# A bidirectional RWKV-7 and latent-attention block: two PSUM banks for each pair of copies in the scan, a scratch of its own for each token tile, and constants later

## The chip, the core and the metric

The kernel runs on one core of a Trainium2 chip. TensorE multiplies, VectorE and ScalarE move results out of PSUM and do elementwise work, GpSimd (POOL) does a little elementwise work, and SyncE (SP) issues the loads of weights. PSUM, where TensorE writes, is used here as eight banks of 128 partitions x 512 float32. The metric is the device time of one execution in microseconds; of a kernel the median of several runs is taken.

## The reference

One encoder layer over 256 tokens of 2048 channels, float32:

```python
h = rms_norm(x, g_pre)
proj = h @ w_in                       # 2048 x 10688
mla_in, rwkv_in, z_mla, z_rwkv, gate_mla, gate_rwkv = split(proj)
# branch 1: latent attention, 8 heads, q and kv through ranks 512
y_mla = mla_attention(q_nope, q_rope, k_nope, k_rope, v_mla)
# branch 2: RWKV-7, 16 heads of 64, one scan forwards and one backwards
rin = rin + rwkv_mu * (centred_shift(rin) - rin)
#   step: sa = st @ a_t; st = st * w_t + sa b_t^T + v_t k_t^T; y = st @ r_t
y = rwkv7_bidir_scan(r, w_f, w_b, k_f, k_b, v, kk, a_f, a_b)
y_rwkv = group_norm(y) + bonus
u_mla = (y_mla * silu(z_mla)) @ w_br_mla
u_rwkv = (y_rwkv * silu(z_rwkv)) @ w_br_rwkv
merged = sigmoid(gate_mla) * u_mla + sigmoid(gate_rwkv) * u_rwkv
x = x + rms_norm(merged @ w_out, g_post)
```

## The kernel before

All large products are made as three products of float32r parts: ScalarE rounds a chunk of weights to its high part (`whi`, L331), VectorE subtracts to get the low part (`wlo`, L334), and TensorE multiplies high by high, high by low and low by high (L400 to L402). A chunk is 128 x 1024 or less; three raw buffers and three split buffers go round. These are the *main matmuls*.

**A planner writes the order.** Nothing is scheduled on the chip: each engine runs its instructions in the order in which they are issued. The order comes from `Streams` (L45), a small simulation. Each part of the kernel is a generator that yields requests such as `("A", cost, ready, table)`, with `P`, `A`, `D`, `G`, `S` for TensorE, ScalarE, VectorE, GpSimd and SyncE. The planner grants the engine that can start first, and among requests that could start within a slot the one with the lowest rank; only then the generator issues its instructions. `W` waits for a condition, `T` for a time. `cA(n)` and `cD(n)` are the costs assumed for n elements on ScalarE and VectorE, `S0` is when loads are assumed to begin, and a yielded number such as `0.73 * n` for a piece of x is an assumed cost. So a changed number changes the order of issue and nothing else. The waits between engines are put in by the framework from the tiles that instructions read and write.

**PSUM.** Three banks (`DB`) serve the main matmuls, five (`MB`) all smaller ones; `take` waits until one is free and `give` returns it.

**The start** (`start`, L1402). x comes in pieces of 256 columns (`dma_stream`, L277). `row(t)` sums the squares of token tile t in four pieces: tile 0 on ScalarE, tile 1 on VectorE (`SQ`), each writing the squares, which nobody reads, to `junk[:, i]`, the same piece for both tiles. Then come sum, root and reciprocal (`rs`), and x is scaled piece by piece on ScalarE, VectorE or GpSimd (`SC`). `turned` transposes x by TensorE, and `ev_h` (L1448) brings each block of h into SBUF in two parts: ScalarE `hhi` (L1452), VectorE `hlo` (L198). The first eight blocks are multiplied unscaled and `ev_first` multiplies by the reciprocals that `spread` laid along the free axis. The constants (four small VectorE operations, L1500 to L1503, which make `vd`, `ka1` and change `vec`) are made as soon as the second reciprocal is there; `mix` (L421) is their first reader.

**The RWKV branch** goes in four quarters Q of four heads, both directions at once, so eight head-states `st`. `front_d`, `front_k`, `front_v` and `bonus` prepare a quarter; `front_d` contains the decay's running sum (`tensor_tensor_scan`, L702). `chunks_of(Q)` (L771) makes the Gram matrices, and inverts a triangular 64 x 64 matrix per chunk of 64 tokens: 32 x 32 blocks on VectorE, then two joins (L856 to L874), each of 32 small matmuls into one bank and four copies of 32 partitions, alternately on ScalarE and VectorE. Then it walks through four chunks q, and in each: `by_v` and the state's products give the right sides in `pu` (one bank; half of the heads on partitions 0 to 63, half on 64 to 127); ScalarE copies the one half (L921) and VectorE the other (L923) into `rhs`; 16 matmuls (L928) solve for U, into `pu` again; ScalarE (L930) and VectorE (L932) copy U into `uv`; then follow the new state (L946), y (L949) and the next chunk's `by_v`. Main matmuls are issued between these steps.

Of the kernel before, what the change touches and what calls it, by code (L numbers as in the profile page):

```python
# [15 lines left out]
S = 256  # L16
D = 2048
# [8 lines left out]
SLOT = {'P': 0.03, 'A': 0.06, 'D': 0.08, 'G': 0.1, 'S': 0.1}  # L26
S0 = 1.5
LATE = 0.3
# [130 lines left out]
def encoder_block_kernel(  # L159
# [117 lines left out]
    def dma_stream():  # L277
# [5 lines left out]
        while True:  # L283
            for what, k, n in before.get(i, ()):
                if what == "x":
                    e = yield ("S", 0.73 * n, 0.0)
                    C = slice(256 * k, 256 * (k + n))
                    nc.sync.dma_start(xt[:, :, C], xv[:, :, C])
                    for kp in range(k, k + n):
                        have["xl", kp] = e  # L290
                else:
                    have["kr", k] = yield ("S", 0.182 * n, 0.0)
                    o = krw[k // 8][:, 0:512].rearrange("p (k c) -> p k c", k=8)
                    nc.sync.dma_start(o[:, k % 8:k % 8 + n], w_in_v[:, k:k + n, 1024:1088])
            yield ("W", lambda: i < len(chunks) and i < done["split"] + NRAW)
            c = chunks[i]
            c.t = yield ("S", 0.55 if i < 2 else 1.1 if i < 9 else 1.46, O.free["D"] if i > 9 else 0.0)
            c.load(raws[i % NRAW])
# [122 lines left out]
    def mix(p, m, mcol, o):  # L421

        q = yield from QP.take()
        for j in range(2):
# [238 lines left out]
    def front_d(Q, d):  # L663
# [36 lines left out]
        act.activation(w65(lw)[:, :, :, 1:65], v4(rv(w2d(th))), AF.Copy, bias=-0.5 * KAPPA, scale=-0.5 * KAPPA)  # L700
        yield ("D", cD(520))
        dve.tensor_tensor_scan(out=fl(th), data0=scanm, data1=fl(lw), initial=0.0, op0=ALU.mult, op1=ALU.add)  # L702
# [68 lines left out]
    def chunks_of(Q):  # L771
# [84 lines left out]
        for step in range(2):  # L856

            m = yield from MB.take()
            pm = m[:, 0:256].rearrange("p (u c) -> p u c", u=8)
            e = yield ("P", 0.5, None, "32x32")  # L860
            for u in range(32):
                j = 32 * (u % 4)
                o = pm[j:j + 32, u // 4]
                if step == 0:
# [3 lines left out]
            for j in range(4):  # L868
                on, cost = (("A", cA(256) + 0.07), ("D", cD(256) + 0.09))[j % 2]
                yield (on, cost, e)  # L870
                copy = act.copy if on == "A" else dve.tensor_copy
                copy(tm[B2, j::4] if step == 0 else Gu[B1, j::4, 32:64], pm[32 * j:32 * j + 32])
            MB.give(m)
            yield ("T", max(O.free["A"], O.free["D"]))  # L874
# [18 lines left out]
        def by_v(pu, q):  # L893

            for dj in range(4):
                for h in range(2):
                    pe.matmul(pu[R64[1 - h], dj], G[:, 2 * dj + h, q, 0:64], z.uv[q][:, 2 * dj + h], start=dj == 0,
                              stop=(dj == 3 and q == 0))

        for q in range(4):  # L900
# [3 lines left out]
            if q == 0:  # L904
                mu = yield from MB.take()
                pu = mu[:, 0:256].rearrange("p (a c) -> p a c", a=4)
                e = yield ("P", 0.48, None, "128x64")
                by_v(pu, q)
            m = yield from MB.take()
            py = m[:, 0:256].rearrange("p (a c) -> p a c", a=4)  # L910
            if q:
                e = yield ("P", 0.5, None, "64x64")

                for dj in range(4):
                    ar = z.ar[dj // 2][:, dj % 2, q]
                    for h in range(2):
                        pe.matmul(pu[R64[1 - h], dj], ar[R64[h], 0:64], Z[R64[h], dj], start=False, stop=dj == 3)
                    for h in range(2):
                        pe.matmul(py[R64[h], dj], Z[R64[h], dj], ar[R64[h], 64:128], start=dj == 0, stop=False)
            e0 = yield ("A", cA(256) + 0.08, e)  # L920
            act.copy(rhs[Hs, 1], pu[R64[0]])  # L921
            e1 = yield ("D", cD(256) + 0.11, e)
            dve.tensor_copy(rhs[Hs, 0], pu[Hs])  # L923
            e = yield ("P", 0.48, max(e0, e1), "64x64")
            for a in range(4):
                for i in range(2):
                    st = 4 * i + a
                    pe.matmul(pu[R64[i], a], G[Hs, st, q, 0:64], rhs[Hs, st % 2, st // 2], start=a == 0, stop=a == 3)  # L928
            e1 = yield ("A", cA(256) + 0.08, e)
            act.copy(uv[Hs, 0:4], pu[R64[0]])  # L930
            e2 = yield ("D", cD(256) + 0.11, e)
            dve.tensor_copy(uv[Hs, 4:8], pu[Hs])  # L932
            MB.give(mu)
            eu = max(e1, e2)
            ez = eu
            Zn = Z
            m2 = (yield from MB.take()) if q < 3 else None
            mu = (yield from MB.take()) if q < 3 else None
            cost = 1.0 if q < 3 else 0.5
# [10 lines left out]
            if q < 3:  # L950
                pu = mu[:, 0:256].rearrange("p (a c) -> p a c", a=4)
                by_v(pu, q + 1)
# [449 lines left out]
    def start():  # L1402
        junk = sb([128, 4, 512], "b8", 1)
        sq = sb([128, 2, 4], "sq")
# [13 lines left out]
        def row(t):  # L1418
            e = []
            for i in range(4):  # L1420
# [74 lines left out]
        O.add(turned([*range(UN // 2, 8), *range(UN // 2)], "x", "h"), 0)  # L1495
        O.add(spread(), 1)
        yield ("W", lambda: ("rs", 1) in have)

        yield ("D", 0.5)
        ts(vd, vec, 0.5, 0.0)  # L1500
        ts(ka1, vd[:, V_KA:V_KA + 8], -1.0, 1.0)
        ts(vec[:, V_MU:V_MUL + 4], vec[:, V_MU:V_MUL + 4], -1.0, 1.0)
        ts(vd[:, V_KK:V_KK + 8], vec[:, V_KK:V_KK + 8], -1.0, 0.0)  # L1503
        yield ("W", lambda: done["dma"] >= 8)
        yield ("A", 0.25, 26.0)
# [147 lines left out]
```

## Time and profile before

| | |
|---|---|
| median of 3 runs | 866.34 us (866.2 to 866.93) |
| profiled execution | 866.99 us |
| its span, first to last instruction | 865.2 us |
| TensorE busy | 843.4 us (97%) |
| VectorE busy | 660.1 us (76%) |
| ScalarE busy | 501.0 us (58%) |
| mean granted TensorE clock | 0.997 of full speed |

Busy is the time in which an engine had an instruction under way. In rows of the trace PE is TensorE, PEld its weight loads, DVE VectorE, ACT ScalarE. `m` and `d` are banks of `MB` and `DB`, and tiles are named without their numbers. A bracket such as `[0.74 <-DVE work L923]` says that the engine stood idle for 0.74 us before the instruction, and what ended that.

### The profile page before, as it was taken

The numbers are of one execution on the slowest core, as the hardware profiler recorded it, in microseconds if no ns is written. First come the engines' busy times: TensorE is split into PE (matmuls) and PEld (weight loads), VectorE is DVE, ScalarE is ACT, GpSimd is POOL, SyncE is SP. The second block draws the span as 40 slices with busy tenths as digits, with TensorE's granted clock in tenths as the row PEclk, the third lists the DMA queues.
The fourth block names the chain that finished last, engine by engine and source line by source line (L and its number), as shares of the span: only waits on it lengthen the run. The fifth ranks groups of instructions, "written<-read, shape, count | busy, mean of one in ns | idle before, by whom it ended". The sixth has DMA issues, their size and how long they took to land.

```text
span 865.2 us, 19404 instructions
## 1 busy us (share of the span) xinstructions
PE 843.4 (97%) x8112; PEld 807.4 (93%) x8112; DVE 660.1 (76%) x1082; ACT 501.0 (58%) x797; POOL 31.8 (4%) x66
## 2 busy tenths in 40 slices
PE   8899999999999999999999999999999999999996
PEld 8899999999999989999999999899999999998884
DVE  5887798869997869887878988766777766765554
ACT  6678654477654587644678444657766543544442
POOL 4210000000000000000010000000000000000000
PEclk9999999999999999999999999999999999999998
DMA  8566646544366624366532566454663575555563
GB/s 273 160 183 169 178 125 183 161 132 123 108 181 185 173 82 117 104 199 178 152 102 77 151 191 174 118 139 159 178 200 112 164 247 191 180 188 193 195 204 113
DMA packets 123528, 139.41 MB, mean 161 GB/s; under 512 B 6704, under 2 KB 110512, under 8 KB 123056
## 3 DMA queue, kind: packets, MB, share of 16 engines
q1 hardware_dynamic: 121664, 135.16, 53.0%
q0 software_dynamic: 768, 1.57, 0.6%
q10 hardware_dynamic: 1008, 1.44, 0.5%
q8 instruction: 63, 1.03, 0.5%
q14 instruction: 25, 0.20, 0.1%
HBM read 136.05 MB, written 2.10 MB: 160 GB/s over the span
## 4 chain that ended last, share of the span: by engine, by line
PE 87%; DVE 7%; ACT 3%; issue 1%; DMA 1%; SPq 0%; POOL 0%; DVEq 0%; ACTq 0%
PE d L400 20%; PE d L402 19%; PE d L401 19%; PE m L1333 2%; PE m L1334 2%; PE m L1335 2%; PE m L801 2%; DVE wlo L334 1%; PE m L402 1%; PE m L400 1%; PE m L401 1%; PE d L1334 1%; PE d L1333 1%; PE d L1335 1%; DVE work L195 1%
## 5 line engine op out<-in xcount | busy, mean ns | idle before, releaser
L331 ACT CAST whi<-raw 128x1024 fp32r<-128x1024 f32 (+3 forms) x252 | 253.1, 1006 | 247.7 <-PE d L401 165.5
L400 PE MATMUL d<-hhi,whi 128*128 128x256 f32 (+1 forms) x1328 | 384.4, 289 | 0.0
L334 DVE TENSOR_TENSOR wlo<-raw,whi 128x1024 fp32r<-128x1024 f32 (+3 forms) x250 | 292.5, 1172 | 116.3 <-ACT whi L331 114.2
L402 PE MATMUL d<-hhi,wlo 128*128 128x256 f32 (+1 forms) x1328 | 375.4, 283 | 1.3 <-DVE wlo L334 1.3
L401 PE MATMUL d<-hlo,whi 128*128 128x256 f32 (+1 forms) x1328 | 375.2, 283 | 0.0
L400 PEld LDWEIGHTS d<-hhi,whi 128*128 128x128 f32 (+1 forms) x1328 | 253.0, 191 | 4.1
L402 PEld LDWEIGHTS d<-hhi,wlo 128*128 128x128 f32 (+1 forms) x1328 | 253.2, 191 | 1.6 <-DVE wlo L334 1.5
L401 PEld LDWEIGHTS d<-hlo,whi 128*128 128x128 f32 (+1 forms) x1328 | 253.4, 191 | 0.1
L195 DVE TENSOR_TENSOR work<-work,work 128x512 f32<-128x512 f32 (+5 forms) x64 | 38.9, 613 | 6.9 <-ACT work L717 2.1
L195 DVE TENSOR_TENSOR u<-u,tmp 128x30 f32<-128x30 f32 (+7 forms) x120 | 29.9, 249 | 3.0
L195 DVE TENSOR_TENSOR tmp<-u 128x30 f32<-128x30 f32 (+7 forms) x120 | 29.8, 249 | 2.7
L402 PE MATMUL d<-uv,wlo 128*128 128x256 f32 x96 | 27.1, 282 | 0.0
L401 PE MATMUL d<-work,whi 128*128 128x256 f32 x96 | 26.9, 280 | 0.0
L400 PE MATMUL d<-uv,whi 128*128 128x256 f32 x96 | 26.8, 279 | 0.0
L1333 PE MATMUL m<-whi,hhi 128*128 128x512 f32 x60 | 23.3, 389 | 0.0
L1334 PE MATMUL m<-wlo,hhi 128*128 128x512 f32 x60 | 23.3, 389 | 0.0
L1335 PE MATMUL m<-whi,hlo 128*128 128x512 f32 x60 | 23.3, 389 | 0.0
L400 PE MATMUL d<-b,whi 128*128 128x256 f32 x80 | 23.0, 288 | 0.0
L402 PE MATMUL d<-b,wlo 128*128 128x256 f32 x80 | 22.6, 282 | 0.0
L401 PE MATMUL d<-ar,whi 128*128 128x256 f32 x80 | 22.4, 280 | 0.0
L195 DVE TENSOR_TENSOR g<-m,mask 128x512 f32<-128x512 f32 x32 | 19.8, 683 | 1.1 <-PE m L801 1.1
L1335 PE MATMUL d<-whi,hlo 128*128 128x512 f32 x48 | 18.7, 389 | 0.0
(331 smaller groups left out, 1451.7 us busy)
## 6 DMA issues: line engine op xcount, KB each, us to landing
raw<-in_w_in_dram SPq DMA_DIRECT2D x160, 512.0 KB, 3.9
raw<-in_w_out_dram SPq DMA_DIRECT2D x32, 512.0 KB, 3.6
raw<-in_w_br_rwkv_dram SPq DMA_DIRECT2D x16, 512.0 KB, 3.4
raw<-in_w_br_mla_dram SPq DMA_DIRECT2D x16, 512.0 KB, 3.4
raw<-in_mla_wkv_b_dram SPq DMA_DIRECT2D x8, 512.0 KB, 3.7
raw<-in_mla_wq_b_dram SPq DMA_DIRECT2D x8, 384.0 KB, 3.5
raw<-in_w_in_dram SPq DMA_DIRECT2D x7, 384.0 KB, 5.3
g<-in_x_dram SPq DMA_DIRECT2D x2, 1024.0 KB, 6.5
```

The costliest lines, as they stand in the source:

```text
L195: dve.tensor_tensor(out=o, in0=a, in1=b, op=op)
L331: act.copy(dst(c.hi), src(raw))
L334: eng.tensor_tensor(out=dst(c.lo), in0=src(raw), in1=dst(c.hi).bitcast(F32), op=ALU.subtract)
L400: pe.matmul(o, hi[:, c:c + m], xhi(k), start=k == k_first and i % 2 == 0, stop=False)
L401: pe.matmul(o, hi[:, c:c + m], xlo(k), start=False, stop=False)
L402: pe.matmul(o, lo[:, c:c + m], xhi(k), start=False, stop=last)
L801: pe.matmul(ms[2 * j + h][:, q * 128:q * 128 + 128], z.kb[R64[h], d, j, q], z.ar[d][R64[h], j, q], start=q == 0, stop=q == 3)
L1333: pe.matmul(banks[t], hhi[:, k, T], hi, start=k == 0, stop=False)
L1334: pe.matmul(banks[t], hhi[:, k, T], lo, start=False, stop=False)
L1335: pe.matmul(banks[t], hlo[:, k, T], hi, start=False, stop=k == KT - 1)
```

## The change

1. `start`: the squares of token tile 0 go to the tile `b8` and those of tile 1 to the tile `u8`.
2. `start`: the four constant operations wait until the last block of h is planned; `mix` waits for them. Two ScalarE copies (`bdr`, `scanm`) that follow them in the same generator come later with them. `spread` has rank 5 where it had 1.
3. `chunks_of`: `pu` is a list of two tiles, each a bank: one for the half of the heads on partitions 0 to 63, one for the other. It takes two banks of `MB` where it took one.
4. Joins: two banks, and ScalarE copies the two pieces of the one bank, VectorE those of the other, instead of alternating in one bank.
5. Numbers of the planner: `S0`, a piece of x, the narrow pieces `kr`, the first two chunks, the joins' copies, and the running sum (1.15 where `cD(520)` gives 0.62).

```diff
-S0 = 1.5
+S0 = 1.75
...
-                    e = yield ("S", 0.73 * n, 0.0)
+                    e = yield ("S", 0.8 * n, 0.0)
...
-                    have["kr", k] = yield ("S", 0.182 * n, 0.0)
+                    have["kr", k] = yield ("S", 0.16 * n, 0.0)
...
-            c.t = yield ("S", 0.55 if i < 2 else 1.1 if i < 9 else 1.46, O.free["D"] if i > 9 else 0.0)
+            c.t = yield ("S", 0.65 if i < 2 else 1.1 if i < 9 else 1.46, O.free["D"] if i > 9 else 0.0)
...
     def mix(p, m, mcol, o):
 
+        yield ("W", lambda: "vd" in have)
...
-        yield ("D", cD(520))
+        yield ("D", 1.15)
         dve.tensor_tensor_scan(out=fl(th), data0=scanm, data1=fl(lw), initial=0.0, op0=ALU.mult, op1=ALU.add)
...
-            m = yield from MB.take()
-            pm = m[:, 0:256].rearrange("p (u c) -> p u c", u=8)
+            ms = []
+            for _ in range(2):
+                ms.append((yield from MB.take()))
+            pms = [m[:, 0:256].rearrange("p (u c) -> p u c", u=8) for m in ms]
...
-                o = pm[j:j + 32, u // 4]
+                o = pms[u % 4 // 2][j:j + 32, u // 4]
...
-                on, cost = (("A", cA(256) + 0.07), ("D", cD(256) + 0.09))[j % 2]
-                yield (on, cost, e)
+                on, cost = (("A", cA(256) + 0.05), ("D", cD(256) + 0.07))[j // 2]
+                yield (on, cost, e if j in (0, 2) else O.free[on])
...
-                    pe.matmul(pu[R64[1 - h], dj], G[:, 2 * dj + h, q, 0:64], z.uv[q][:, 2 * dj + h], start=dj == 0,
+                    pe.matmul(pu[1 - h][R64[1 - h], dj], G[:, 2 * dj + h, q, 0:64], z.uv[q][:, 2 * dj + h], start=dj == 0,
...
-            act.copy(rhs[Hs, 1], pu[R64[0]])
+            act.copy(rhs[Hs, 1], pu[0][R64[0]])
             e1 = yield ("D", cD(256) + 0.11, e)
-            dve.tensor_copy(rhs[Hs, 0], pu[Hs])
+            dve.tensor_copy(rhs[Hs, 0], pu[1][Hs])
...
-            act.copy(uv[Hs, 0:4], pu[R64[0]])
+            act.copy(uv[Hs, 0:4], pu[0][R64[0]])
             e2 = yield ("D", cD(256) + 0.11, e)
-            dve.tensor_copy(uv[Hs, 4:8], pu[Hs])
-            MB.give(mu)
+            dve.tensor_copy(uv[Hs, 4:8], pu[1][Hs])
+            MB.give(*mu)
...
-            mu = (yield from MB.take()) if q < 3 else None
+            mu = []
+            for _ in range(2 if q < 3 else 0):
+                mu.append((yield from MB.take()))
...
-        junk = sb([128, 4, 512], "b8", 1)
+        junks = [sb([128, 4, 512], n, 1) for n in ("b8", "u8")]
...
-            e = []
+            e, junk = [], junks[t]
...
-        O.add(spread(), 1)
+        O.add(spread(), 5)
         yield ("W", lambda: ("rs", 1) in have)
+        yield ("W", lambda: ("h", KT - 1) in have)
 
         yield ("D", 0.5)
         ts(vd, vec, 0.5, 0.0)
...
+        have["vd"] = True
```

## Rows read from the trace of the kernel before

**Rows 1.** The page's first part: busy time of each engine, its share, instructions

```profile
PE 843.4 (97%) x8112; PEld 807.4 (93%) x8112; DVE 660.1 (76%) x1082; ACT 501.0 (58%) x797; POOL 31.8 (4%) x66
```

**Rows 2.** Stretches: length, busy time of each engine, clock, DMA share, GB/s

```profile
20.00:30.00 10.00, 7.26 (x61) 6.78 (x61) 9.10 (x21) 6.86 (x19) 6.16 (x9) 1.00 0.62 194
30.00:40.00 10.00, 10.00 (x88) 10.00 (x86) 8.15 (x13) 6.55 (x14) 1.03 (x1) 1.00 0.45 119
...
850.00:866.00 16.00, 7.15 (x31) 5.42 (x29) 7.39 (x16) 1.97 (x6) 0.00 (x0) 0.84 0.37 131
```

**Rows 3.** Timeline of TensorE, 20 to 30 us: start, duration, what, idle before

```profile
23.80 1.31 PE L1464 MATMUL m<-iv,g 128*128 128x128 f32 x10 [1.81 <-DVE g L1446]
...
26.35 0.66 PE L1464 MATMUL m<-iv,g 128*128 128x128 f32 x4 [0.79 <-DVE hlo L198]
```

**Rows 4.** Waits of TensorE: us in total, times, longest

```profile
PE m L928 <- DVE work L923: 2.0, 5, 0.7
...
PE m L592 <- DVE work L195: 1.4, 4, 0.7
PE d L402 <- DVE wlo L334: 1.3, 1, 1.3
...
PE m L946 <- ACT uv L930: 1.0, 1, 1.0
```

**Rows 5.** Timeline of VectorE, 17 to 24 us

```profile
17.48 0.84 DVE L1428 SCALAR_TENSOR_TENSOR b<-g 128x512 f32<-128x512 f32 x1 [0.99 <-ACT b L1425]
...
20.82 0.65 DVE L201 TENSOR_SCALAR vd<-iv 128x124 f32<-128x124 f32 x1
...
23.07 0.67 DVE L1446 TENSOR_SCALAR g<-g,rs 128x512 f32<-128x512 f32 x1
```

**Rows 6.** Timeline of VectorE and of ScalarE, 33 to 42 us

```profile
33.85 0.88 DVE L198 SCALAR_TENSOR_TENSOR hlo<-m,iv,hhi 128x256 fp32r<-128x256 f32 x2 [0.15 <-ACT hhi L1452]
...
41.04 0.90 ACT L426 ACTIVATE qpad<-work,vd 96x256 f32<-96x256 f32 x2
```

**Rows 7.** Waits of VectorE and ScalarE for each other's copies: us, times, longest

```profile
DVE work L923 <- ACT work L921: 14.8, 10, 3.3
...
ACT u L872 <- DVE u L872: 3.6, 4, 1.5
...
DVE uv L932 <- ACT uv L930: 3.1, 5, 1.5
```

**Rows 8.** Timeline of a step of the scan, 427 to 430 us

```profile
427.58 0.28 PE L688 MATMUL m<-tw,work 96*128 96x256 f32 x1
...
428.35 0.36 ACT L921 COPY work<-m 64x256 f32<-64x256 f32 x1
...
428.75 0.43 DVE L923 COPY work<-m 64x256 f32<-64x256 f32 x1 [1.06 <-ACT work L921]
...
429.23 0.68 PE L928 MATMUL m<-work,g 64*64 64x64 f32 x16 [0.74 <-DVE work L923]
...
429.80 0.47 ACT L693 ACTIVATE work<-m,vd 128x256 f32<-128x256 f32 x1
```

**Rows 9.** Timeline of another step of the scan, 305 to 307 us

```profile
305.23 0.36 ACT L921 COPY work<-m 64x256 f32<-64x256 f32 x1
...
305.63 0.43 DVE L923 COPY work<-m 64x256 f32<-64x256 f32 x1 [0.65 <-ACT work L921]
...
306.11 0.68 PE L928 MATMUL m<-work,g 64*64 64x64 f32 x16 [0.46 <-DVE work L923]
```

**Rows 10.** The running sums as a group (busy, mean ns), and one solve's wait

```profile
L702 DVE TENSOR_TENSOR_SCAN work<-scanm,work 128x520 f32<-128x520 bf16 x8 | 9.9, 1238 | 3.9 <-ACT work L700 3.8
...
211.03 0.68 PE L928 MATMUL m<-work,g 64*64 64x64 f32 x16 [0.26 <-DVE work L923]
```

**Rows 11.** Timeline of VectorE and of TensorE between scan and attention

```profile
583.40 0.68 DVE L195 TENSOR_TENSOR b<-work,b 128x512 fp32r<-128x512 f32 x1
...
595.25 0.28 PE L1084 MATMUL d<-b,whi 128*128 128x256 f32 x1
```

More of the change, by code (lines that the diff above doesn't have):

```diff
@@ L868, in chunks_of @@
             for j in range(4):
-                on, cost = (("A", cA(256) + 0.07), ("D", cD(256) + 0.09))[j % 2]
-                yield (on, cost, e)
+                on, cost = (("A", cA(256) + 0.05), ("D", cD(256) + 0.07))[j // 2]
+                yield (on, cost, e if j in (0, 2) else O.free[on])
                 copy = act.copy if on == "A" else dve.tensor_copy
-                copy(tm[B2, j::4] if step == 0 else Gu[B1, j::4, 32:64], pm[32 * j:32 * j + 32])
-            MB.give(m)
+                copy(tm[B2, j::4] if step == 0 else Gu[B1, j::4, 32:64], pms[j // 2][32 * j:32 * j + 32])
+            MB.give(*ms)
             yield ("T", max(O.free["A"], O.free["D"]))
@@ L904, in chunks_of @@
             if q == 0:
-                mu = yield from MB.take()
-                pu = mu[:, 0:256].rearrange("p (a c) -> p a c", a=4)
+                mu = []
+                for _ in range(2):
+                    mu.append((yield from MB.take()))
+                pu = [t[:, 0:256].rearrange("p (a c) -> p a c", a=4) for t in mu]
                 e = yield ("P", 0.48, None, "128x64")
@@ L916, in chunks_of @@
                     for h in range(2):
-                        pe.matmul(pu[R64[1 - h], dj], ar[R64[h], 0:64], Z[R64[h], dj], start=False, stop=dj == 3)
+                        pe.matmul(pu[1 - h][R64[1 - h], dj], ar[R64[h], 0:64], Z[R64[h], dj], start=False, stop=dj == 3)
                     for h in range(2):
@@ L927, in chunks_of @@
                     st = 4 * i + a
-                    pe.matmul(pu[R64[i], a], G[Hs, st, q, 0:64], rhs[Hs, st % 2, st // 2], start=a == 0, stop=a == 3)
+                    pe.matmul(pu[i][R64[i], a], G[Hs, st, q, 0:64], rhs[Hs, st % 2, st // 2], start=a == 0, stop=a == 3)
             e1 = yield ("A", cA(256) + 0.08, e)
-            act.copy(uv[Hs, 0:4], pu[R64[0]])
+            act.copy(uv[Hs, 0:4], pu[0][R64[0]])
             e2 = yield ("D", cD(256) + 0.11, e)
-            dve.tensor_copy(uv[Hs, 4:8], pu[Hs])
-            MB.give(mu)
+            dve.tensor_copy(uv[Hs, 4:8], pu[1][Hs])
+            MB.give(*mu)
             eu = max(e1, e2)
@@ L937, in chunks_of @@
             m2 = (yield from MB.take()) if q < 3 else None
-            mu = (yield from MB.take()) if q < 3 else None
+            mu = []
+            for _ in range(2 if q < 3 else 0):
+                mu.append((yield from MB.take()))
             cost = 1.0 if q < 3 else 0.5
@@ L950, in chunks_of @@
             if q < 3:
-                pu = mu[:, 0:256].rearrange("p (a c) -> p a c", a=4)
+                pu = [t[:, 0:256].rearrange("p (a c) -> p a c", a=4) for t in mu]
                 by_v(pu, q + 1)
```

## The prediction

> **What bounds the kernel now.** I read the engine totals first: TensorE is busy 843.4 of 865.2 us, the next engine 76% [rows 1]. So the end moves only by what TensorE's own stream loses, 865.2 - 843.4 = 21.8 us of idle, and a faster VectorE or ScalarE counts only where TensorE stood waiting for it. The table of stretches says where: from 850 us to the span's end at 865.2 TensorE is busy 7.15 us, so 8.05 us of the idle lie at the tail, which nothing here touches; the stretch from 20 to 30 us has 7.26 of 10 [rows 2]. TensorE's timeline shows what that is: 1.81 us until a VectorE scaling of x and 0.79 us until a VectorE eviction [rows 3]. The list of TensorE's waits holds the middle: its four largest make 2.0 + 1.4 + 1.3 + 1.0 = 5.7 us, of which 2.0 in five waits stand in front of U's solve (L928), the product behind the copies that the change takes apart [rows 4]. The others are for VectorE or ScalarE coming late through their queues. What can be gained is therefore about 2.6 + 5.7 us, and nothing by a shorter scan as such: main matmuls fill TensorE between its steps.
>
> **Start: constants and the spread later.** VectorE does the four constant operations from 20.82 us, then two 128x128 ones of the spread, and only at 23.07 the scaling for which TensorE stands [rows 5]. The change moves the four behind the last transposed h, and gives the spread rank 5. Taken out, the scaling can start 23.07 - 20.82 = 2.25 us sooner; it takes 0.67 and ends at 21.49, before TensorE runs dry at 23.80 - 1.81 = 21.99 [rows 3, 5]. Gain 1.8 us. If two more pieces of that 0.67 us stood in between, it would end at 22.83 and about 1.0 us would be left; I take 0.5 us as the lower bound, for one more such piece and a bit. The 0.79 us gap waits for an eviction of h, some 0.44 us each on VectorE (two in 0.88), which is busy 9.10 of 10 us there [rows 2, 3, 6]. Deferring 2.25 us of its work helps, but the spread still has to be done among these evictions; I take half, 0.4 us, bounds 0 and 0.8.
>
> Where do the deferred pieces lie? The first consumer of the constants is ScalarE's scaling in `mix` at 41.04 us [rows 6], and the new wait stands in front of it. Behind it queue the tanh, the low-rank products and with them the fronts of quarter 0. The last eviction of h ends at 33.85 + 0.88 = 34.73 us, so the constants, less than the 2.25 us of all six, have some 6 us of cover, in a stretch where TensorE is busy 10 of 10 [rows 2, 6]; with the cover gone, each us late would move the fronts by one, which still have main matmuls beside them. The two ScalarE copies behind the constants (block matrix and scan mask) and the spread's consumers come later still. Cost: nothing.
>
> **Start: one scratch per token tile.** The last square on VectorE waited 0.99 us for ScalarE's square of the other tile, because both write the same piece of scratch [rows 5]. That wait goes. What is late next is ScalarE's own last square, so the two sums come under 1 us sooner, at a time when TensorE still has matmuls of the first task. I count zero; it is a reserve for the 1.8 us above. The second scratch is the tile that quarter 0's front fills tens of us later.
>
> **Scan and U: a bank for each half.** Before, VectorE's copy of the right sides waited for ScalarE's copy out of the same bank, 10 times of 16, 14.8 us in all; U's copies 3.1 us, and a join's copies alternate the same way, 3.6 us [rows 7]. One such place shows the price: ScalarE copies at 428.35 for 0.36, VectorE starts at 428.75, takes 0.43, and TensorE starts at 429.23 after 0.74 us of idle [rows 8]. With two banks VectorE, free for 1.06 us by then, runs first, and TensorE waits only for ScalarE, until about 428.71 + 0.05: it was free at 428.49, so 0.27 is left and 0.47 is gained. At 305 us: ScalarE ends at 305.59, VectorE had been free 0.65 us, TensorE free at 305.65; all 0.46 us goes [rows 9]. Together 0.9 us. The rest of the five waits is put down to a VectorE that came late for other reasons, where no bank helps. Bounds: 0, if these two merely meet another delay, and 2.0, if all five go [rows 4]. The joins cost TensorE no idle row of its own; they are shorter chains, zero.
>
> The Trainium skill, PSUM — Partial Sum Buffer, section on bank collisions, says that two engines may be in one bank at the same time if they are in different quadrants of 32 partitions. The two copies here read partitions 0 to 63 and 64 to 127, so by that rule the machine needed no second bank, and the term would be 0 and the sum 0.9 us smaller. The rows of before speak for the program: VectorE starts 0.03 to 0.04 us after ScalarE's end at both places, which is what a program that orders by tile or bank does [rows 8, 9].
>
> **The planner's numbers.** The rest changes only the order in which the same instructions are written. One correction is large: the decay's running sum is planned at 0.62 us and takes 1.238; now it is planned at 1.15 [rows 10]. Behind one of these VectorE's copy came late and TensorE stood 0.26 us at 211.03 [rows 10]: gain 0.25, bounds 0 and 0.26. What stays of the four is 5.7 - 0.9 - 0.25 = 4.55 us, waits that a new order draws anew. Less of VectorE's queue is blocked (14.8 + 3.1 + 3.6 us of standing still less), and the plan is nearer to the durations, so I take a seventh of it as gained, 0.65 us; bounds all of it gained, or half as much again lost (2.3).
>
> **Sum.** 1.8 + 0.4 + 0 + 0.9 + 0.25 + 0.65 = 4.0 us. The profiled execution took 866.99 us, 1.8 around its span of 865.2: 862.99. It stands 0.65 above the median of the runs, 866.34, so for the median I forecast 866.34 - 4.0 = 862.3 us. What a measurement of this kernel can tell from no change is about 0.2%, 1.7 us: 864.6 and 868.1 are the borders.
>
> **Rivals.** (a) *Most of the middle's waits go too.* If the waits were mostly knock-on of the blocked queues and of the short plan, the 4.55 go whole: 866.34 - (1.8 + 0.8 + 0.9 + 0.25 + 4.55) = 858.0. For it: VectorE's 14.8 us of waiting [rows 7]. Against it: one of the four is itself a wait for a split of weights (1.3 us), which is not touched [rows 4]. Chance of under 860.5: 0.14.
>
> (b) *The gain of the start is only put off.* VectorE at 9.10 of 10 us may be what paces the h phase [rows 2]; then removing 2.25 us in front shows as a second gap 3 us later, and the middle's new waits cancel the other gains. Left is 0.9 + 0.25: 865.2. Against (b): from 30 us on TensorE is full while VectorE has 1.85 us in 10 free. Chance of 864.6 to 868.1: 0.18.
>
> (c) *Banks run short; slower.* The scan now holds up to four of five banks at a hand-over (y, state and two for the next right sides) where it held three. A front's low-rank product holds one from 427.58 until ScalarE has read it, 430.27 at the earliest, 2.69 us [rows 8]. There are 12 hand-overs; if each waited that long, the chain of quarters would be 32.3 us longer, less the 21.5 us of waits that go [rows 7]. It decides from the point where quarter 3 is later than its cover: the last split of the normed kv piece ends at 584.08, and its first product is at 595.25, so 11.2 us [rows 11]. Without the give-back, 32.3 - 11.2 = 21.1 us would come on top: 866.34 - 4.0 + 21.1 = 883.4; with it (10.8 us) it stays inside the cover. A few hand-overs with other users can't reach it. No such gap, repeated step by step, is in the list of before [rows 4]. Chance of over 868.1, by this or by an order with new waits: 0.08.
>
> (d) *The split of the banks doesn't do what it is for.* If VectorE's copy stood behind ScalarE's for another reason than the bank (both wait for the same product, and ScalarE's end 0.03 us ahead would be chance), the pairs stay as they are and 0.9 goes out of the sum: 866.34 - 3.1 = 863.2. The rows speak against it, with 10 of 16 copies behind ScalarE's [rows 7]. The page named above gives it its other ground, that the machine needs no second bank. Chance 0.08; its time lies within the forecast's borders.
>
> **How the numbers follow.** The forecast's case, 860.5 to 864.6, has 0.52, and (d) beside it 0.08; (a) 0.14; (b) 0.18; (c) 0.08. The range leaves about 0.07 of (a) below 858.8 and about 0.12 above 866.2. Faster by over 0.2% is 0.52 + 0.08 + 0.14 = 0.74, within it 0.18, slower 0.08. The likeliest case's own range is 860.5 to 864.6.
>
> **What would show it.** In the start, VectorE's scaling right behind the reciprocals, the constants after 34 us, and TensorE's stretch from 20 to 30 us at 9.3 or more of 10. In the scan, VectorE's copy no longer led by ScalarE's (14.8 us to under 2), and waits in front of the solve of 1 us or less. In the plan, running sums no longer followed by a late copy. Wrong would be: the same idle in the start under another releaser; four largest waits of the middle of 6 us or more in sum; waits of the first right sides' or state's products for evictions of other streams' banks, or the first kv product waiting for its split.

## The result and the profile after

The changed kernel takes 856.43 us (median of 4 runs, 855.62 to 857.1) where the kernel before took 866.27 in the same series (4 runs): a ratio of 0.9887, 95% interval 0.987 to 0.9904. The gain is 9.8 us; forecast were 4.0, and the time lies below the range of 858.8 to 866.2. The sign was right, and so was TensorE as the engine that sets the end; the size was not. The profiled execution took 856.67, with a span of 854.9 us.

The engine totals of the kernel after (busy time, share, instructions):

```profile
PE 840.6 (98%) x8112; PEld 807.5 (94%) x8112; DVE 658.7 (77%) x1082; ACT 499.8 (58%) x797; POOL 31.5 (4%) x66
```

Against [rows 1], TensorE's idle went from 21.8 to 14.3 us, 7.5 less, and with the same 8112 matmuls its busy time fell by 2.8 as well. The waits of TensorE in the kernel after (us in total, times, longest), which answer to [rows 4]; here L933 is the solve (L928 before), L593 the second of the head sums (L592), L1471 the transposing of x (L1464), and the first line stands in the kernel before too:

```profile
PE m L1420 <- POOL ones L254: 1.1, 1, 1.1
PE m L1471 <- DMA g<-in_x_dram: 1.0, 1, 1.0
PE d L401 <- DVE hlo L198: 0.9, 2, 0.7
PE m L933 <- DVE work L928: 0.7, 3, 0.4
PE m L811 <- DVE g L195: 0.6, 1, 0.6
PE m L593 <- DVE work L195: 0.5, 2, 0.3
```

The 2.0 us before the solve are 0.7, the 1.4 before the head sums 0.5, and the waits for a split of weights (1.3) and for U's copy (1.0) are gone whole.

**Where in the kernel.** The 5460 matmuls that read a split of weights (`whi` or `wlo`) come in the same order in both, so they serve as a ruler: the time at which the n-th starts, before less after, is what was gained by then. At the 151st, the end of the start, it is 35.00 - 33.17 = 1.83 us; at 290 us 1.89; after quarter 1's stretch 375.37 - 369.20 = 6.17; after quarter 2's 9.35; after quarter 3's 10.35; at the last 10.23. So the middle, from the 151st to the last, gave 8.4 us, all of it in quarters 1 to 3 of the scan. Stretches between the same main matmuls, each called by the quarter whose walk ends in it (length, busy time of each engine, clock, DMA share, GB/s), first before, quarters 1, 2 and 3:

```profile
290.07:375.37 85.30, 81.93 (x1045) 77.25 (x1043) 72.19 (x111) 55.85 (x96) 4.18 (x9) 1.00 0.42 118
375.37:495.50 120.13, 117.46 (x1344) 113.00 (x1343) 99.52 (x166) 73.78 (x113) 3.22 (x8) 1.00 0.50 141
495.50:583.51 88.01, 87.36 (x1070) 84.06 (x1069) 68.66 (x129) 45.07 (x70) 0.61 (x2) 1.00 0.56 154
```

and after:

```profile
288.18:369.20 81.02, 80.49 (x1044) 76.90 (x1043) 72.22 (x112) 55.41 (x96) 4.18 (x9) 1.00 0.45 127
369.20:486.15 116.95, 116.13 (x1345) 112.61 (x1343) 97.90 (x160) 72.30 (x112) 3.27 (x8) 1.00 0.50 141
486.15:573.17 87.02, 87.02 (x1071) 84.16 (x1069) 69.12 (x133) 45.96 (x70) 0.61 (x2) 1.00 0.58 162
```

Quarter 1's stretch is 4.28 us shorter, but only 3.37 - 0.53 = 2.84 of that is idle: 1.44 us came out of time in which TensorE counts as busy, with the same matmuls done. Over the three it is 8.45 us of length, 6.69 - 1.35 = 5.34 of idle and 3.1 of busy time. That the clock is 1.00 in all six says that it is no matter of the clock.

**The start.** VectorE after (start, duration, what, idle before); [rows 5] show the same work before:

```profile
16.38 1.76 DVE L1435 SCALAR_TENSOR_TENSOR u<-g 128x512 f32<-128x512 f32 x1
...
20.63 0.95 DVE L1453 TENSOR_SCALAR g<-g,rs 128x512 f32<-128x512 f32 x1
...
29.02 0.22 DVE L201 TENSOR_SCALAR vd<-iv 128x124 f32<-128x124 f32 x1
```

and the stretch that [rows 2] gave with 7.26 us of TensorE:

```profile
20.00:30.00 10.00, 9.16 (x75) 8.66 (x76) 9.31 (x24) 8.28 (x22) 5.37 (x7) 1.00 0.76 244
```

The scaling starts at 20.63, 2.44 us sooner, and the constants stand at 29.02. They are not behind the last block of h but behind the point at which it is *planned*, and nobody waits for them: `mix`, their first reader, runs at 39.21.

### The profile page after: what moved, and what is told of

Read it like the earlier page. It is cut to its first block, busy times and chain, and to the rows that moved or that the text cites. A ratio compares the mean times of both kernels' runs of the same rounds, so it can differ in the third digit from the quotient of the medians.

```text
span 854.9 us, 19432 instructions
## 1 busy us (share of the span) xinstructions
PE 840.6 (98%) x8112; PEld 807.5 (94%) x8112; DVE 658.7 (77%) x1082; ACT 499.8 (58%) x797; POOL 31.5 (4%) x66
## 3 DMA queue, kind: packets, MB, share of 16 engines
q10 hardware_dynamic: 1008, 1.44, 0.5%
## 4 chain that ended last, share of the span: by engine, by line
PE 86%; DVE 6%; ACT 4%; issue 1%; DMA 1%; POOL 0%; SPq 0%; DVEq 0%; ACTq 0%
PE d L400 19%; PE d L401 18%; PE d L402 18%; PE m L1340 2%; PE m L1341 2%; PE m L1342 2%; PE m L802 2%; DVE wlo L334 2%; DVE work L195 1%; PE m L402 1%; PE m L400 1%; PE m L401 1%; PE d L1340 1%; PE d L1341 1%; PE d L1342 1%
## 5 line engine op out<-in xcount | busy, mean ns | idle before, releaser
L1340 PE MATMUL d<-whi,hhi 128*128 128x512 f32 x48 | 18.7, 389 | 0.0
```

The source lines that it names most:

```text
L1340: pe.matmul(banks[t], hhi[:, k, T], hi, start=k == 0, stop=False)
```

## Experiments

Each result is a median of five rounds beside the kernel before, which took 865.7 to 865.95 us in these series. "In the middle" is the gain by the ruler above from the 151st main matmul to the last, read from one profiled execution; below half a us it says nothing. Two more readings of the traces are used. How far an edit changes the order of issue is counted by the names of tiles, instruction by instruction, on each engine; between before and after, 1752 of TensorE's 8112 places differ. And where small products were put further back, the ruler runs ahead of the work done; this is said where it matters. The start scatters by more: the nine kernels here that begin in the order of the kernel before reach the 151st main matmul between 33.28 and 35.00 us, the seven that begin as the kernel after between 32.29 and 33.17, as x lands sooner or later (in the nine TensorE waits 0.5 to 2.2 us for it in front of the transposing).

### The parts, each put into the kernel before by itself

**Scan's banks alone** (`chunks_of` takes two banks for `pu`, all else as before).

```diff
...
-                mu = yield from MB.take()
-                pu = mu[:, 0:256].rearrange("p (a c) -> p a c", a=4)
+                mu = []
+                for _ in range(2):
+                    mu.append((yield from MB.take()))
+                pu = [t[:, 0:256].rearrange("p (a c) -> p a c", a=4) for t in mu]
...
```

> The kernel before with the two banks of the scan alone; joins, squares, constants and the planner's numbers as before. Theory A (banks): the start stays at its 1.8 us more, the middle gains 5 to 7 us, so 859 to 861.5. Theory B (plan): 864.5 to 866.5. The prediction's term for the banks, 0.9 us: 865.4.

863.74 us (ratio 0.9971 to 0.999), 2.58 in the middle: neither theory's time. The order is nearly the old one, with 62 of TensorE's 8112 places changed, two of VectorE's and none of ScalarE's. VectorE's wait for ScalarE's copy is gone; the solve waits 1.0 + 0.3 us where it waited 2.0 (L930 is the solve here, TensorE's waits):

```profile
PE m L592 <- DVE work L195: 1.7, 5, 0.7
PE d L402 <- DVE wlo L334: 1.3, 1, 1.3
...
PE m L930 <- DVE work L925: 1.0, 3, 0.4
...
PE m L930 <- ACT work L923: 0.3, 1, 0.3
```

At the prediction's two places it came as forecast: 0.28 us is left of the 0.74 and nothing of the 0.46. The wait of 1.0 us for U's copy has no row any more either.

**The running sum's planned length alone.**

```diff
-        yield ("D", cD(520))
+        yield ("D", 1.15)
         dve.tensor_tensor_scan(out=fl(th), data0=scanm, data1=fl(lw), initial=0.0, op0=ALU.mult, op1=ALU.add)
```

> The kernel before with one number changed: the running sum planned at 1.15 us instead of 0.62. If the plan's truth about it is what counts, the middle gains 2.5 to 4 us by it alone and loses the 1.3 us wait for a split and most of the 1.4 us of waits of the head sums: 862 to 863.5. The prediction's term, 0.25 us: 865.7. Rival, that the plan needs the banks for it to help: 865 to 866.5.

860.91 us (0.9926 to 0.995), 5.28 in the middle, more than the 2.5 to 4 expected: one number of the planner, and half of the whole gain. It changes 2539 of TensorE's 8112 places. At the end of quarter 3's stretch the ruler reads 7.51 us, with 16 products of y not yet done; some 2 us are lost again behind it, where the new order's attention waits 0.9 us for VectorE (L1208) in place of 0.3. The waits for U's copy and for the split of weights go, though the scan still has one bank and VectorE still waits for ScalarE. TensorE's waits, then VectorE's:

```profile
PE m L928 <- DVE work L923: 1.7, 4, 0.6
...
PE m L592 <- DVE work L195: 1.0, 3, 0.5
```

```profile
DVE work L923 <- ACT work L921: 13.0, 9, 3.2
```

**The start's edits alone** (scratch per tile, constants and spread later).

```diff
+        yield ("W", lambda: "vd" in have)
...
-        junk = sb([128, 4, 512], "b8", 1)
+        junks = [sb([128, 4, 512], n, 1) for n in ("b8", "u8")]
...
-        O.add(spread(), 1)
+        O.add(spread(), 5)
         yield ("W", lambda: ("rs", 1) in have)
+        yield ("W", lambda: ("h", KT - 1) in have)
...
```

> The kernel before with the start's edits alone: a scratch for each token tile, constants and spread later, loads planned as before. The prediction's term, 1.8 + 0.4 us: 863.8, with TensorE's 1.8 us wait for the scaling gone. Rival, that the start's gain comes from the loads' planned times: 865.5 to 866.

864.77 us (0.9974 to 0.9991), 0.23 in the middle. TensorE's 1.8 us before the transposing are gone, and its wait for the eviction of h is 1.1 where it was 0.8; the 151st main matmul comes at 33.86.

**The numbers of the loads alone.**

```diff
-S0 = 1.5
+S0 = 1.75
...
-                    e = yield ("S", 0.73 * n, 0.0)
+                    e = yield ("S", 0.8 * n, 0.0)
...
```

> The kernel before with the planned times of the loads alone (when they begin, a piece of x, the narrow pieces, the first chunks). By the prediction nothing: 866 within 0.7, with the 1.8 us wait for the scaling still there. Rival: the order in which the first products and transposes stand against the second piece of x changes, and 1 us or more goes: 865 or less.

864.31 us (0.997 to 0.9988), nothing in the middle (0.25 lost). The start's order shifts: TensorE stands 2.1 us for ScalarE's scaling instead of 1.8 for VectorE's. The gain over before is in the median and not in the one profile, so where it lies stays open.

**The joins alone** (two banks, the two copies of a bank on one engine, new costs).

```diff
...
-                on, cost = (("A", cA(256) + 0.07), ("D", cD(256) + 0.09))[j % 2]
-                yield (on, cost, e)
+                on, cost = (("A", cA(256) + 0.05), ("D", cD(256) + 0.07))[j // 2]
+                yield (on, cost, e if j in (0, 2) else O.free[on])
...
```

> The kernel before with the joins' two banks and their costs alone. By the prediction zero: 866 within 0.7. Rival, any new order of issue moves the middle by a us or more either way: below 865 or above 867.

864.14 us (0.9966 to 0.9986), 3.06 in the middle. That a part without an idle row of its own gains 3 us was against my sum. Nor is it a new order: TensorE's 8112 and ScalarE's 797 places are all as before, and VectorE has two of its splits elsewhere. What is gone is ScalarE's wait for VectorE's copies, the line of [rows 7] and its fellow of the second join, in the kernel before:

```profile
ACT g L872 <- DVE g L872: 3.4, 4, 1.2
```

so 3.6 + 3.4 = 7.0 us in which ScalarE's queue stood. One such place in the kernel before, on ScalarE:

```profile
425.96 0.36 ACT L872 COPY g<-m 32x256 f32<-32x256 f32 x1 [0.74 <-DVE g L872]
...
427.29 1.04 ACT L331 CAST whi<-raw 128x1024 fp32r<-128x1024 f32 x1
```

From there ScalarE works without a pause to its copy of the right sides at 428.35, for which VectorE waits, and after it TensorE, 0.74 us [rows 8]. The same step with the joins alone, on ScalarE and TensorE:

```profile
422.11 0.75 ACT L874 COPY g<-m 32x256 f32<-32x256 f32 x2 [0.55 <-PE m L869]
...
424.88 0.36 ACT L923 COPY work<-m 64x256 f32<-64x256 f32 x1
...
425.89 0.68 PE L930 MATMUL m<-work,g 64*64 64x64 f32 x16
```

TensorE has no wait there. The other place that the prediction prices, 0.46 us at 306.11, is gone as well; in the kernel before ScalarE had stood 0.73 us at 301.77 for VectorE's copy in the join.

Alone, the five gain 2.2 + 5.0 + 1.2 + 1.6 + 1.8 = 11.8 us by their medians, together 9.8. They overlap in part: TensorE's wait of 1.0 us for U's copy, for one, is gone with the scan's banks alone and with the sum's number alone. Behind quarter 3 the number alone also loses what the five together keep.

### Order held, banks taken back

The next two issue exactly the order of the kernel after, on every engine, with the second bank taken and given back but not used, so that only what an engine waits for differs. In the first, the line stands at two places.

```diff
-                pu = [t[:, 0:256].rearrange("p (a c) -> p a c", a=4) for t in mu]
+                pu = [mu[0][:, 0:256].rearrange("p (a c) -> p a c", a=4) for t in mu]
```

> The changed kernel's order of issue on every engine, with both halves of the right sides and of U put back into one bank (the second bank is still taken, and stays empty). Theory A, the second bank itself removes the middle's idle: VectorE's copy waits for ScalarE's again 8 or more times of 16, and 4 to 7 us of the 8.4 us won after 50 us come back, so 860.5 to 863.5. Theory B, the new order (better planned costs) removes it: at most 1.5 us come back, 856.4 to 858.

857.42 us (0.9889 to 0.9914), 1.27 lost in the middle. VectorE's waits of this kernel:

```profile
DVE work L928 <- ACT work L926: 14.3, 9, 3.1
...
DVE uv L937 <- ACT uv L935: 4.1, 4, 2.1
```

So of 18.4 us that VectorE stands still, 1.27 reach TensorE. The next run, of the same series and the same order, has 855.87 us, 1.55 less, and their runs do not overlap.

The joins likewise:

```diff
-            pms = [m[:, 0:256].rearrange("p (u c) -> p u c", u=8) for m in ms]
+            pms = [ms[0][:, 0:256].rearrange("p (u c) -> p u c", u=8) for m in ms]
```

> The changed kernel's order, with the joins' 32 products put back into one bank (the second is taken and empty). Theory A for the joins, that their two banks are worth something: 1 us or more comes back, 857.5 or above. The prediction's term, zero, since a join's copies end no wait of TensorE: 856.4 within 0.7.

855.87 us (0.9871 to 0.9897), 0.12 gained in the middle: the joins' second bank is worth nothing. The same edit in the order of the kernel with the joins alone:

> The order of the run with the joins' edit alone, with the joins' products back in one bank. If the joins' 3.1 us in the middle came from the order that the edit brings: 864.1 within 0.7, the middle within 0.3 of that run's. If from the two banks: 866 to 867.

863.11 us (0.996 to 0.9986), 2.62 in the middle where that kernel had 3.06, a little outside both figures expected. So the second bank gives little of the 3.06, and a new order can't give it, since there is none. What is left of the edit is who copies which pieces. Alternating in one bank, the two engines wait for each other from piece to piece; two pieces of ScalarE and then two of VectorE leave one hand-over, and of the waits between the two in the joins one line is left in this run:

```profile
DVE g L874 <- ACT g L874: 1.1, 3, 0.7
```

### The running sum: its length, its plan, or any other plan

**Taken back in the kernel after** (planned 0.62 again).

> The changed kernel with the running sum planned at 0.62 us again; another order, the same instructions and banks. Theory A (banks): 856 to 858. Theory B (the plan's truth about the running sum is what counts): 859 to 862, with copies late behind running sums.

860.18 us (0.9921 to 0.9945), 3.61 lost in the middle. The order is nearly that of the kernel before (114 of TensorE's 8112 places differ), so the 8.4 us split: 4.80 come from banks and joins in nearly the old order, 3.61 from the number on top of them. Two of the large waits are back as they were before:

```profile
PE m L593 <- DVE work L195: 1.5, 4, 0.7
PE d L402 <- DVE wlo L334: 1.3, 1, 1.3
```

**The order of before, the sum itself short.** The number may count because the sum ends late and stops ScalarE's queue, or because it redraws the order.

```diff
-        dve.tensor_tensor_scan(out=fl(th), data0=scanm, data1=fl(lw), initial=0.0, op0=ALU.mult, op1=ALU.add)
+        dve.tensor_tensor_scan(out=fl(th)[:, 260:520], data0=scanm[:, 260:520], data1=fl(lw)[:, 260:520], initial=0.0, op0=ALU.mult, op1=ALU.add)
```

> The kernel before, the same order on every engine, with the running sum over the second half of its columns only (the first half is left out, so the decays are not the reference's): it now takes about what the plan says, 0.62 us. Theory D, that the plan's shortfall is what makes instructions come late: the middle gains 2 to 5 us with nothing reordered, so 861 to 864, and the waits of ScalarE's exp for it (5.8 us in all) shrink to under 2. Theory E, that any new order would do because the old one was unlucky: the order is the old one, so under 1 us beyond the 8 sums' direct share, 865 or more.

863.65 us (0.9968 to 0.9987), 1.70 in the middle, less than the 2 to 5 expected. The half takes 694 ns, near the planned 0.62, and ScalarE's wait for it falls from 5.8 us to:

```profile
ACT work L705 <- DVE work L702: 2.7, 4, 0.8
```

So in this order the lateness costs some 1.7 us and not 5.28. The same in the order of the kernel after:

> The changed kernel's order with the running sum over the second half of its columns only (the first half is left out). If the planned 1.15 us had covered the sum's lateness, making it shorter gives nothing more, under 0.5 us: 856 to 857. If lateness is left, 855 or less.

855.52 us (0.9867 to 0.9901), 0.66 in the middle: there little lateness was left to save.

**Other planned lengths in the kernel before**, and another number as a control (the head sums', 0.476 made 0.52).

> The kernel before with the running sum planned shorter still, 0.35 us: a new order further from the truth. Theory D: no gain, 865.5 or above. Theory E: a new draw, 861 to 865 more likely than not.

> The kernel before with the running sum planned longer than it takes, 1.8 us against 1.24. Theory D: as with 1.15 or a little less gained, since nothing behind it comes later than planned: 860.5 to 863. Theory E: a new draw, anywhere from 861 to 867.

> The kernel before with another number of the plan moved a little, the head sums' four matmuls at 0.52 us instead of 0.476, which makes nothing truer: a new order of the middle. Theory D: 866 within 1.5. Theory E: 861 to 864.5.

Planned 0.35: 864.70 us (0.9977 to 0.9994), 0.23 in the middle; the time is theory E's, but what it gained lies in the start. Planned 1.80: 860.35 (0.9922 to 0.9946), 5.78. The other number: 865.74 (0.999 to 1.0009), 0.10. The other number is a weak control, with 98 of TensorE's 8112 places changed; 0.35 changes 1649 and gains as little. So it isn't that any new order is better, and it isn't that the truth is best: from 0.62 to 1.15 comes the step, and half as much again as the truth loses nothing. TensorE's waits with 1.80, in the kernel before with its single banks:

```profile
PE m L928 <- DVE work L923: 0.6, 4, 0.2
PE m L592 <- DVE work L195: 0.4, 2, 0.2
PE d L402 <- DVE wlo L334: 0.3, 1, 0.3
```

**Room for everything, by another number.** `LATE` is a lateness that the planner adds to when inputs are ready.

```diff
-LATE = 0.3
+LATE = 0.6
```

> The kernel before with one other number: the margin by which the planner puts small products behind their planned inputs 0.6 us instead of 0.3. If what a longer planned sum gives is mostly room between a small product's inputs and the product, this gives 2 to 5 us too: 861 to 864. If it is the truth about the sum's place in VectorE's queue, 865 or more, with ScalarE's exp still waiting 5 us or more for it.

869.76 us (1.0031 to 1.0061). By the end of quarter 2's stretch the ruler shows 12.94 us gained from the 151st main matmul on; 52 small products stand further back there, some 5.6 us at their pace in the kernel before, so the gain is estimated at 7.3 us, about as much as the change had. Then quarter 3's chain was too long, its cover of main matmuls ran out, and all came back. The stretch, with the first two of TensorE's long waits:

```profile
575.00:600.00 25.00, 17.80 (x277) 16.06 (x274) 15.44 (x31) 12.48 (x26) 0.61 (x2) 0.80 0.20 64
```

```profile
585.12 0.68 PE L928 MATMUL m<-work,g 64*64 64x64 f32 x16 [3.15 <-DVE work L923]
586.30 1.16 PE L946 MATMUL m<-uv,b 128*64 128x64 f32 x16 [0.51 <-ACT uv L930]
```

The kernel before has TensorE busy all 25 us of this stretch at 1.00.

> The changed kernel with the margin at 0.6 us. By room: the 2 us of waits left in the middle shrink by half, 855 to 856. By the truth alone: 856.4 within 0.7.

868.26 us (1.0013 to 1.0035), 12.4 lost in the middle: in the kernel after the same number is 0.8 us ahead at the end of quarter 1's stretch, and quarter 3 runs dry in the same way.

**Two more lengths in the kernel after.**

> The kernel after, with the running sum planned at its measured length, 1.24 us, where it has 1.15. If what counts is that the plan holds the true length, this is the best of the three sizes (1.15, 1.24, 1.80): 855.5 to 856.5 us, and the middle not behind the kernel after's. If the sizes only draw one order or another, it comes out anywhere within about 1.5 us of 856.4.

> The kernel after, with the running sum planned at 1.80 us, half as much again as it takes. If it is room behind the sum that pays, whatever its true length: 855.5 us or less, TensorE's waits in the middle below those of the kernel after. If it is the true length that pays, and more only moves the quarter's chain later: 857 us or more. In the old order, 1.80 was 0.5 us ahead of 1.15 in the middle.

Planned 1.24, the measured length: 855.97 us (855.69 to 856.26; ratio 0.9869 to 0.9898). Planned 1.80: 855.34 us (854.88 to 855.41; 0.9858 to 0.9891), 1.17 ahead of the kernel after in the middle. The runs of these two, taken side by side, do not overlap, so the longer plan is a little ahead; whether by its room or by the order that it draws is not shown. 1.80 has the best time of all here, by 1.1 us (0.13%) over the kernel after, which was timed in another series, and that is within what a measurement can tell from no change.

## Why the prediction was wrong

**The step that failed first is the running sum's term**: "Behind one of these VectorE's copy came late and TensorE stood 0.26 us at 211.03 [rows 10]: gain 0.25, bounds 0 and 0.26." It measured 5.28 us alone and 3.61 taken back. I looked only behind the sum on VectorE's own queue. The wait on the other side was in the list of ScalarE's waits in the kernel before, and I did not price it:

```profile
ACT work L705 <- DVE work L702: 5.8, 6, 1.4
```

ScalarE's exponential needs the sum; it blocks ScalarE's queue, and behind it stand the splits of weights and U's copy. One place in the kernel before, on three engines:

```profile
312.63 0.43 DVE L923 COPY work<-m 64x256 f32<-64x256 f32 x1 [3.07 <-ACT work L921]
...
313.09 1.25 DVE L702 TENSOR_TENSOR_SCAN work<-scanm,work 128x520 f32<-128x520 bf16 x1
...
314.43 0.64 ACT L705 ACTIVATE work<-work 128x520 f32<-128x520 f32 x1 [1.18 <-DVE work L702]
314.97 1.03 ACT L331 CAST whi<-raw 128x1024 fp32r<-128x1024 f32 x1
316.03 0.36 ACT L930 COPY uv<-m 64x256 f32<-64x256 f32 x1
...
316.44 0.91 PE L946 MATMUL m<-uv,b 128*64 128x64 f32 x16 [1.04 <-ACT uv L930]
```

The sum ends at 314.34, 0.63 later than with its planned length, ScalarE stands 1.18, splits, copies U, and TensorE stands 1.04: the whole row for L946 in [rows 4], which I had put to "waits that a new order draws anew". But the sum has only a part in it. With the half sum in the same order the row is

```profile
PE m L946 <- ACT uv L930: 0.5, 1, 0.5
```

and with the scan's banks alone, the sum as long and planned as short as before, it is gone: there VectorE doesn't stand the 3.07 us for ScalarE's copy of the right sides, and the sum begins at 311.02.

Lateness is the smaller part of the number's worth. The half sum shows 1.7 us for the lateness itself; the rest of the 3.6 to 5.3 is order. Planned longer, the sum leaves VectorE free later in the plan, and later products are placed behind more main matmuls; their inputs can then be ready when TensorE comes to them. The traces show the places: quarter 2's last product of y stands behind 2922 main matmuls in the kernel before, with 0.35 and with the number taken back, behind 2946 with 1.15 in the old kernel, 2958 in the kernel after, 2964 with 1.80 in either. The two runs with a longer plan than the truth, and the lateness of 0.6 up to the end of quarter 2, speak for room rather than truth, but do not prove it. Which product's place brings how much was not tried, and that 1.15, 1.24 and 1.80 are all good could still hold luck in the draw.

**The joins' zero failed too**: "The joins cost TensorE no idle row of its own; they are shorter chains, zero." By themselves they gave 3.06 us in the middle, in the old order. I took 3.6 us of waits for a join's copies, which is the first join's row, where both have 7.0, and looked for idle rows of TensorE before the joins' own products; the 7.0 us stood in ScalarE's queue, behind which other products' inputs wait. With the joins alone, the solve waits 0.8 us where it waited 2.0, and the two waits priced for the scan's banks are gone without a second bank for the scan: they had two causes, and the prediction saw one.

**The budget was too small as well.** "What can be gained is therefore about 2.6 + 5.7 us" took TensorE's waits at their rows. The middle gave 8.4 us, of which idle is 807.75 - 800.18 = 7.57 before less 799.35 - 796.40 = 2.95 after, 4.6; another 3.8 was busy time. Of what it may consist, the pace of main matmuls in the kernel after shows (TensorE's timeline):

```profile
479.79 0.28 PE L401 MATMUL d<-hlo,whi 128*128 128x256 f32 x1
479.91 0.28 PE L402 MATMUL d<-hhi,wlo 128*128 128x256 f32 x1
```

Each takes 0.28 us by the profile, which models the ends of matmuls, but the next starts 0.12 behind it. In front of a wait the last one has nothing behind it, so 0.28 - 0.12 = 0.16 us more are lost in time that counts as busy. With 14 waits of over 0.12 us in the middle before and 9 after, that makes 0.8 us of the 3.8. Starts alone show more: some 2.4 us, an estimate from starts that come over 0.06 us later than the median of their pair of shapes, went at starts that were late without an idle row, 287 before and 267 after. The rest was not traced.

**Point by point.** *The constants*: 1.8 + 0.4 forecast for the start. The pair of profiles gives 1.83, but the means of the nine and the seven kernels named above 34.18 - 32.78 = 1.40; the 20 to 30 us stretch has 9.16 of 10, just under the 9.3 set. With the 8.4 of the middle that makes the 9.8. The 0.4 for the eviction's gap did not come: TensorE waits 0.9 us for evictions of h after. The start's edits alone, at 33.86, are 0.3 ahead of the nine, less than their scatter; by their medians they gave 1.2 and the loads' numbers 1.6, more together than the 1.4, so what of it is whose stays open. The constants' place was wrong (29 us, not after 34), their cost of nothing right. *The scratch* at nothing: right; VectorE no longer waits for ScalarE's square, and the sums of the squares begin 0.18 us sooner. *The scan's banks*: 0.9 forecast with bounds 0 and 2.0; 1.27 in the new order, 2.58, above the bound, in one that is nearly the old; the two places gave what was forecast, and U's copy, 1.0 us, which was not priced, went too. *The joins' banks* at zero: right, below half a us in either order; who copies which piece was not, as said above. *A seventh of the remaining waits*: most of them went.

**The rivals.** (a) came nearest, 858.0, and both causes that it names carried: the unblocked queues of scan and joins 4.80 us in nearly the old order, the number of the sum 3.61 on top, or 5.28 by itself. It had a chance of 0.14. Its ground against itself, that the wait for the split of weights is not touched, was false: that wait goes with the running sum's number alone and returns when the number is taken back. (b) did not happen: the start's gain is kept to the end. (c) did not happen: after the change the last split of the normed kv piece ends at 574.57 and the first product is at 584.9, so the cover is still 10 us; its mechanism, a chain longer than its cover, is what the lateness of 0.6 shows. (d) is refuted: with two banks VectorE's copy no longer waits for ScalarE's at all, and with one bank in the same order it waits 14.3 us. The Trainium skill, PSUM — Partial Sum Buffer, section Terms, gives a hardware ground on which no second bank would be needed, different quadrants of one bank being open to two engines at once. The runs can't show whether the chip would allow it here; they show that this program waits by the bank, and that in the scan this costs 1.27 us in the new order and 2.58 in nearly the old.

## What to carry to other kernels

Where a planner writes the order, an operation planned too short is to be priced on every engine that waits for it, with what is queued behind each of those waits: here 0.26 us on its own queue and some 1.7 in all. What the corrected plan gives beyond that, to 3.6 or 5.3, comes from the order, and only a run shows it. Two engines that copy by turns out of one bank, in a program that waits by the bank, stop each other's queues, and that can cost TensorE time in front of products that have nothing to do with the copies: here 3.06 us. Idle time before a matmul was less than what the wait cost in this kernel, since the drain in front of it counts as busy. And more room in the plan pays only up to the cover of the longest chain: the number that gained some 7.3 us by quarter 2 ended 4.1 us behind the kernel before, when quarter 3 outlived its main matmuls.

## What the runs showed of the hardware

The granted clock follows a starved TensorE: in the stretch from 575 to 600 us, where waits of 3.15, 0.51, 0.98, 0.51 and 1.90 us stood between short products, its mean was 0.80 of the full 2.4 GHz (0.75 in the kernel after with the same number), so part of it ran at the level of 1.2 GHz; before, with TensorE busy throughout, it was 1.00. So starvation costs more than its idle rows.

One of VectorE's squares of 128x512 in the kernel after took 1.76 us (at 16.38), another 0.68 (at 15.19), both while GpSimd ran a subtraction from 15.23 to 17.59. The Trainium skill, GPSIMD Engine Reference, section Specifications, says that GpSimd shares its SBUF interfaces with VectorE, with contention for VectorE instructions that have two inputs in SBUF, as a square by x times x has. The longer square agrees with that; the shorter, which began 0.04 us before the subtraction, doesn't show it, so the cause is open.
